# Retention queries and keys as block products, four group-norm roots at once on VectorE, and the output transposes in the next stage

## The chip, the cores and the metric

The kernel runs on one core of a Trainium2 chip. A core has TensorE (PE: matmuls and transposes, results in PSUM), VectorE (DVE), ScalarE (ACT), GpSimd (POOL) and SyncE (SP, which here only issues transfers); each works off a queue of its own in order, and semaphores join them. 16 DMA engines move data between HBM and the on-chip memory (SBUF). The metric is the time of one execution in microseconds of the device, smaller is better.

## The reference

Two layers of a hybrid decoder on 512 tokens of width 1024. Each layer has one combined input projection, dilated window attention in three groups, retention with four heads, sigmoid gates, an output projection and a SwiGLU block, with a LayerNorm after each half. What the change touches is retention:

```python
z = jnp.einsum('bsd,dc->bsc', x, w_in) + b_in          # q_r, k_r: 4 heads x 256 columns each
def rot(t):
    t1, t2 = t[..., :half], t[..., half:]
    return jnp.concatenate([t1 * cos - t2 * sin, t1 * sin + t2 * cos], axis=-1)
q = rot(q); k = rot(k) * (dk ** -0.5)
...
# o: per head a causal product of decayed scores (q k^T) with v, 512 columns a head
mu = jnp.mean(o, axis=-1, keepdims=True)
var = jnp.mean(jnp.square(o - mu), axis=-1, keepdims=True)
return (o - mu) * lax.rsqrt(var + GN_EPS)
...
y_b = jax.nn.silu(g_r) * y_r
```

## The kernel before

Every float32 operand of a large product is split into a high and a low part of a shorter format (`hilo`, L92: ScalarE casts the high part, VectorE subtracts to get the low part), and a product is three matmuls (`mm3`, L84): high by high, high by low, low by high. The activations x stand transposed in `xh` and `xl`, eight blocks of 128 rows by 512 tokens. Weights come in raw tiles of 128 x 1024 (`rawp`, eight of them, L64), loaded from the SyncE queue (L110, L211), and are split into pairs `whi`, `wlo` (`wp`, four pairs, L61).

Most projections are block products: the activations, the weights and the result are cut into 2 x 2 blocks, and seven products of sums of blocks do the work of eight. `Right` (L306) prepares the weight side: it loads B11, B21, B22 and the sums P1 = B11 + B12 and P3 = B12 + B22, whose second summand is added in flight by an accumulating transfer from GpSimd's queue (L321); P2 and P4 are made from P1 on VectorE (L347). The high parts are cast by ScalarE (L330) one product ahead, the low parts made by VectorE (L336). The sums of x for the left side stand in `xs`. `wide` (L406) runs the seven products with weights stationary and 256 tokens moving, into three PSUM tiles that `ev` empties; the merge gates of the layer (`gates`, L921) and most of the FFN use it. `tall` (L377) does the same with x stationary and 512 columns moving; the retention values and output gates of a head come from it through `biased` (L458).

Retention queries and keys were left as a plain product: `rotary(h)` (L657) loads two weight tiles each for q and k, multiplies with 512 tokens moving (`wstat`, L233), forms the products with the cosine and sine tables straight from PSUM (L668), adds them (L672, L673) and splits the result.

The stages of a head follow each other in the loop at L890: `rotary(h)`, then `ret_values_gates(h)`. Beside them run small jobs from a list, `side`: `pace(us)` spreads what is in the list over so many microseconds of matmuls, `tick` (L134) takes jobs out as the matmuls are written, and `drain` writes the rest. The scores of head h (`ret_scores`, L836) are side jobs of its values stage; its outputs (`ret_outputs`, L856) are side jobs of the next head's rotary stage, or of `gates` for the last head. One output job multiplies scores with values, takes mean and variance (L868, L869), the root (`rstd_of`, L120: a power on GpSimd and one Newton step on VectorE), subtracts the mean and multiplies by the gate (L872), and scales by the root on ScalarE (L873). A turn job transposes the four 128 x 128 parts on TensorE (L878), copies them out (L880) and writes them to HBM from ScalarE's queue (L881). `y_load` reads them back in the last call of `gates`.

The order in which instructions stand on an engine's queue is set when the program is built, by a planner that goes through the program with estimated durations and takes, when an engine is free, the earliest written instruction that is ready. So a weight's low part can stand ahead of an eviction that is written before it.

Of the kernel before, what the change touches and what calls it, by code (L numbers as in the profile page):

```python
# [10 lines left out]

F32 = mybir.dt.float32
F32R = mybir.dt.float32r
AF = mybir.ActivationFunctionType
ALU = mybir.AluOpType
PSUM = bass.MemoryType.PSUM
# [2 lines left out]
P = 128  # L19
# [3 lines left out]
NI = S // P  # L23
# [9 lines left out]
RQ = 256  # L33
# [4 lines left out]
C_QR = 3 * AW  # L38
C_KR = C_QR + RH * RQ
# [5 lines left out]
EPS = 1e-5  # L45
# [8 lines left out]
def hybrid_kernel(ctx, tc, x, rel_bias, w_in, b_in, w_attn_proj, w_ret_proj, w_out,  # L54
# [3 lines left out]
    pe, act, dve, pool = nc.tensor, nc.scalar, nc.vector, nc.gpsimd  # L58
# [25 lines left out]
    def mm3(ps, ah, al, bh, bl, start, stop):  # L84
        mm(ps, ah, bh, start, False)
        mm(ps, ah, bl, False, False)
        mm(ps, al, bh, False, stop)
# [4 lines left out]
    def hilo(src, hi, lo):  # L92
        act.copy(out=hi, in_=src)  # L93
        dve.tensor_tensor(out=lo, in0=src, in1=hi.bitcast(F32), op=ALU.subtract)  # L94
# [4 lines left out]
    def work(name):  # L99
        return wk.tile([P, S], F32, tag="w2", name=name)  # L100
# [4 lines left out]
    def view(t, a, b):  # L105
        return t[:, :a * b].rearrange("p (a b) -> p a b", a=a)
# [13 lines left out]
    def rstd_of(var):  # L120
        ve = sm.tile([P, 1], F32, tag="ve", name="ve")
        y = sm.tile([P, 1], F32, tag="ry", name="ry")
        t = sm.tile([P, 1], F32, tag="rt", name="rt")
        dve.tensor_scalar(ve, var, EPS, None, op0=ALU.add)
        pool.tensor_tensor(out=y, in0=ve, in1=mhalf, op=ALU.pow)  # L125
        dve.scalar_tensor_tensor(out=t, in0=y, scalar=ve, in1=y, op0=ALU.mult, op1=ALU.mult)
        dve.tensor_scalar(t, t, -0.5, 1.5, op0=ALU.mult, op1=ALU.add)
        dve.tensor_tensor(out=y, in0=y, in1=t, op=ALU.mult)
        return y


# [10 lines left out]
    def pace(us):  # L142
        rate[0], credit[0] = len(side) / us, 0.0
# [57 lines left out]
    def pair_units(w, c, c2=None):  # L201

        vs = []
        for hf in range(2):
            ks = slice(4 * hf, 4 * hf + 4)
            if c2 is None:
                vs.append(load(w[:, ks, c:c + 256], 4, 256))
            else:
                vs.append(view(raw(), 4, 256))
                for q, cc in enumerate((c, c2)):  # L210
                    nc.sync.dma_start(vs[hf][:, :, q * P:(q + 1) * P], w[:, ks, cc:cc + P])  # L211
        return [unit(v) for v in vs]
# [20 lines left out]
    def wstat(us, q):  # L233

        need(*range(NI))
        ps = psum("ps")
        for k in range(KD):
            h, l = part_of(us, k, q)
            mm3(ps, h, l, xh[:, k], xl[:, k], k == 0, k == KD - 1)
            tick(STEP)  # L240
        return ps
# [395 lines left out]
    def layer(ly, cp):  # L637
# [4 lines left out]
        def bcol(c):  # L642
            return bT[:, c // P:c // P + 1]
# [10 lines left out]
        def slot(name="op", dt=F32R):  # L654
            return opp.tile([P, 2, S], dt, tag="op", name=name)

        def rotary(h):  # L657

            rot = []
            for c0 in (C_QR + h * RQ, C_KR + h * RQ):  # L660
                us = pair_units(w_l, c0)
                prod = []
                for t in range(2):
                    ps = wstat(us, t)
                    pr = []
                    for tb in (cos, sin):
                        m = work("rp")
                        dve.scalar_tensor_tensor(out=m, in0=ps, scalar=bcol(c0 + t * P), in1=tb, op0=ALU.add, op1=ALU.mult)  # L668
                        pr.append(m)
                    prod.append(pr)  # L670
                (t1c, t1s), (t2c, t2s) = prod
                dve.tensor_tensor(out=t1c, in0=t1c, in1=t2s, op=ALU.subtract)  # L672
                dve.tensor_tensor(out=t1s, in0=t1s, in1=t2c, op=ALU.add)  # L673
                pair = []
                for src in (t1c, t1s):
                    o_ = slot("rot")
                    hilo(src, o_[:, 0], o_[:, 1])
                    pair.append(o_)
                rot.append(pair)
            heads[h]["q"], heads[h]["k"] = rot  # L680

        def ret_values_gates(h):
            cv, cg = C_VR + h * RV, C_GR + h * RV
            vr = heads[h]["v"] = [None] * NI
            gs = heads[h]["g"] = [None] * NI
            pairs = {}

            def left(i, ps, s):
                if s is not None:
                    dve.tensor_tensor(out=s, in0=ps, in1=s, op=ALU.add)  # L690
                vr[i] = slot("vr")
                hilo(ps if s is None else s, vr[i][:, 0], vr[i][:, 1])

            def gate(i, t):
                if i // 2 not in pairs:
                    pairs[i // 2] = slot("gs", F32)
                gs[i] = pairs[i // 2][:, i % 2]
                act.activation(out=gs[i], in_=t, func=AF.Silu)

            yield from biased(halves(w_l, 0, (2, 2), cv, cg, RV), RV, ly * RH + h, left, gate)  # L700
# [134 lines left out]
        with stage("ret") as rp:  # L835
            def ret_scores(h):  # L836

                dec = rp.tile([P, S], F32, tag="dec", name="dec")
                pool.dma_start(dec, c_dec[h])
                heads[h]["p"] = [rp.tile([P, 2, S - j * P], F32R, tag=f"p{j}", name="pj") for j in range(NI)]  # L840

                def one(j):
                    n = S - j * P
                    ps = psum()[:, :n]
                    for d in range(2):
                        k_, q_ = heads[h]["k"][d], heads[h]["q"][d]
                        mm3(ps, k_[:, 0, j * P:(j + 1) * P], k_[:, 1, j * P:(j + 1) * P],
                            q_[:, 0, j * P:], q_[:, 1, j * P:], d == 0, d == 1)
                    t = work("pt")
                    dve.tensor_tensor(out=t[:, :n], in0=ps, in1=dec[:, :n], op=ALU.mult)  # L850
                    sl = heads[h]["p"][j]
                    hilo(t[:, :n], sl[:, 0], sl[:, 1])

                return [lambda j=j: one(j) for j in range(NI)]

            def ret_outputs(h):  # L856

                ys = {}

                def one(i):  # L860
                    po = psum()
                    for j in range(i + 1):
                        sl, o = heads[h]["p"][j], (i - j) * P
                        vr = heads[h]["v"][j]
                        mm3(po, sl[:, 0, o:o + P], sl[:, 1, o:o + P], vr[:, 0], vr[:, 1], j == 0, j == i)
                    st = sm.tile([P, 6], F32, tag="st", name="st")
                    mv = sm.tile([P, 2], F32, tag="mv", name="mv")
                    dve.bn_stats(out=st, in_=po)  # L868
                    dve.bn_aggr(out=mv, in_=st)  # L869
                    rs = rstd_of(mv[:, 1:2])  # L870
                    y = ys[i] = rp.tile([P, RV], F32, tag="yb", name="yb", bufs=4)
                    dve.scalar_tensor_tensor(out=y, in0=po, scalar=mv[:, 0:1], in1=heads[h]["g"][i], op0=ALU.subtract, op1=ALU.mult)  # L872
                    act.mul(out=y, in_=y, mul=rs)  # L873

                def turn(i):
                    px = psum()
                    for t in range(NI):
                        pe.transpose(px[:, t * P:(t + 1) * P], ys[i][:, t * P:(t + 1) * P], ident)  # L878
                    o_ = work("yt")
                    act.copy(out=o_, in_=px)  # L880
                    act.dma_start(y_d[h * RV:(h + 1) * RV, i * P:(i + 1) * P].rearrange("(t p) s -> p t s", p=P),  # L881
                                  o_.rearrange("p (t s) -> p t s", t=NI))

                ops = [lambda i=i: one(i) for i in range(NI)]
                tr = [lambda i=i: turn(i) for i in range(NI)]
                n = [nothing]
                return ops[:1] + n * 2 + ops[1:2] + n * 2 + ops[2:3] + tr[:1] + n * 2 + ops[3:] + tr[1:2] + n * 3 \
                    + tr[2:3] + n * 4 + tr[3:]

            for h in range(RH):  # L890
                if h:
                    pace(20)
                    rotary(h)
                    drain()
                    vg = ret_values_gates(h)
                side.extend([nothing] * (8 if h else 1) + ret_scores(h))
                pace(14 if h == 0 else 30)
                run(vg)
                drain()
                side.extend(ret_outputs(h))  # L900


            wa_l, wr_l = rows(w_attn_proj[ly]), rows(w_ret_proj[ly])
# [302 lines left out]
```

## Time and profile before

| what | us |
|---|---|
| three runs | 2182.38, 2186.73, 2186.76; median 2186.73 |
| profiled execution, its own time | 2185.52 |
| span of its profile | 2183.7 |

The three retention heads with a rotary stage of this kind take, in layer 0, the time from 288.35 to 508.88 us of the span; layer 1 repeats it about 1080 us later. The profile's windows give, for a stretch of time, how long each engine was busy (with the number of instructions), the clock granted to TensorE as a share of full speed, the share of time that the DMA engines were busy, and GB/s. The timeline gives start, duration, engine, line, operation, output and inputs of each instruction, and in brackets how long the engine had been idle before it and what ended that. The chain of waits is followed back from the last instruction. A matmul's duration in a row is longer than its spacing from the next, since matmuls are pipelined.

### The profile page before, as it was taken

To read this page: it belongs to the slowest core of one execution; us is meant where nothing else is said; L and a number is where in the kernel's file an instruction comes from. 1 tells how busy PE (TensorE), PEld (TensorE's weight loads), DVE (VectorE), ACT (ScalarE), POOL (GpSimd) and SP (SyncE) were. 2 spreads that over 40 slices of the span, in tenths; PEclk is the share of its full clock that TensorE was granted. 3 is DMA by queue.
4 is the path that set the end of the run, shared out by engine and by line. 5 is a ranking of instruction groups with operands and counts; after the bars stand their busy time and mean duration, and the time that the engine had idled before them with its cause. 6 is when DMAs were issued, how large, how long until landed. Compare 5 with 4: busy or idle time off the path is not lost.

```text
span 2183.7 us, 32442 instructions
## 1 busy us (share of the span) xinstructions
PE 2161.5 (99%) x12906; PEld 1902.4 (87%) x12906; DVE 1396.0 (64%) x2011; ACT 980.6 (45%) x1585; POOL 228.3 (10%) x253
## 2 busy tenths in 40 slices
PE   8999999999999999999999999999999999999998
PEld 7977788889988899989898778888899889999996
DVE  5643677777755685747675346767877447766575
ACT  4444544546633263525245445444556233544350
POOL 4100011011000100010020000111010001000001
PEclk9999999999999999999999999999999999999999
DMA  8944266458685356656269343565577762666551
GB/s 230 235 134 104 59 164 164 135 131 194 190 305 192 88 154 132 171 133 158 93 163 255 89 92 92 140 178 148 137 188 227 260 193 58 175 151 161 125 161 39
DMA packets 304954, 338.60 MB, mean 155 GB/s; under 512 B 21790, under 2 KB 243138, under 8 KB 304673
## 3 DMA queue, kind: packets, MB, share of 16 engines
q1 hardware_dynamic: 227712, 248.81, 37.8%
q0 software_dynamic: 49808, 74.90, 18.1%
q10 hardware_dynamic: 27280, 12.80, 2.1%
q8 instruction: 101, 1.65, 0.3%
q14 instruction: 53, 0.43, 0.1%
HBM read 310.67 MB, written 28.53 MB: 155 GB/s over the span
## 4 chain that ended last, share of the span: by engine, by line
PE 90%; issue 4%; DMA 3%; DVE 2%; POOL 1%; ACT 0%; SPq 0%; POOLq 0%; DVEq 0%; ACTq 0%
PE ps L82 81%; PE px L82 7%; DMA raw<-in_w_in 2%; PE px L546 1%; DMA exd<-wb 1%; PE px L878 1%; POOL ry L125 0%; DMA mb<-exd 0%; DMA exd<-pk 0%; PE px L170 0%; DVE xtok L1001 0%; DVE wlo L336 0%; ACT whi L330 0%; PE px L602 0%; DVE xtok L1010 0%
## 5 line engine op out<-in xcount | busy, mean ns | idle before, releaser
L336 DVE TENSOR_TENSOR wlo<-raw,whi 128x1024 fp32r<-128x1024 f32 (+1 forms) x364 | 417.9, 1150 | 214.1 <-ACT whi L330 212.9
L82 PE MATMUL ps<-xh,whi 128*128 128x256 f32 (+1 forms) x1536 | 516.6, 338 | 4.5 <-ACT whi L93 3.5
L330 ACT CAST whi<-raw 128x1024 fp32r<-128x1024 f32 (+1 forms) x364 | 359.0, 990 | 345.4 <-PE ps L82 205.3
L82 PE MATMUL ps<-xh,wlo 128*128 128x256 f32 (+1 forms) x1536 | 500.9, 327 | 1.0 <-DVE wlo L94 1.0
L82 PE MATMUL ps<-xl,whi 128*128 128x256 f32 (+1 forms) x1536 | 501.2, 327 | 0.2 <-DVE xl L94 0.2
L82 PE MATMUL ps<-xs,whi 128*128 128x256 f32 (+1 forms) x2048 | 404.6, 296 | 0.0
L82 PEld LDWEIGHTS ps<-xs,whi 128*128 128x128 f32 x2048 | 327.7, 191 | 10.3
L94 DVE TENSOR_TENSOR wlo<-raw,whi 128x1024 fp32r<-128x1024 f32 (+2 forms) x162 | 193.3, 1196 | 202.0 <-ACT whi L93 201.0
L82 PEld LDWEIGHTS ps<-xh,whi 128*128 128x128 f32 x1536 | 292.4, 191 | 34.3 <-issue 5.7
L82 PEld LDWEIGHTS ps<-xh,wlo 128*128 128x128 f32 x1536 | 292.9, 191 | 26.5 <-DVE wlo L94 1.2
L82 PEld LDWEIGHTS ps<-xl,whi 128*128 128x128 f32 x1536 | 293.7, 191 | 19.5 <-DVE xl L94 1.0
L82 PE MATMUL ps<-xs,wlo 128*128 128x256 f32 (+1 forms) x1024 | 303.4, 296 | 0.0
L93 ACT CAST whi<-raw 128x1024 fp32r<-128x1024 f32 (+2 forms) x162 | 166.0, 1027 | 240.8 <-PE ps L82 150.7
L82 PE MATMUL ps<-whi,xs 128*128 128x512 f32 (+1 forms) x768 | 219.6, 360 | 0.6 <-ACT whi L330 0.4
L82 PEld LDWEIGHTS ps<-xs,wlo 128*128 128x128 f32 x1024 | 196.0, 191 | 5.0
L82 PE MATMUL ps<-whi,ht 128*128 128x512 f32 x576 | 178.4, 389 | 0.0
L82 PEld LDWEIGHTS ps<-whi,xs 128*128 128x128 f32 x768 | 137.7, 188 | 21.1 <-ACT sn L466 1.0
L82 PE MATMUL ps<-wlo,xs 128*128 128x512 f32 (+1 forms) x384 | 138.1, 360 | 0.8 <-DVE wlo L336 0.8
L321 POOL DMA_DIRECT2D raw<-in_w_in x64 | 79.2, 1263 | 472.9 <-DMA raw<-in_w_in 159.8
L82 PEld LDWEIGHTS ps<-whi,ht 128*128 128x128 f32 x576 | 108.2, 188 | 22.3
L321 POOL DMA_DIRECT2D raw<-in_w_ffn_gate x40 | 51.8, 1295 | 679.4 <-DMA raw<-in_w_ffn_up 251.4
L347 DVE TENSOR_TENSOR raw<-raw 128x1024 f32<-128x1024 f32 (+1 forms) x104 | 119.5, 1149 | 2.7 <-DMA raw<-in_w_in 0.5
(183 smaller groups left out, 2897.0 us busy)
## 6 DMA issues: line engine op xcount, KB each, us to landing
raw<-in_w_in SPq DMA_DIRECT2D x152, 512.0 KB, 4.3
raw<-in_w_ffn_up SPq DMA_DIRECT2D x64, 512.0 KB, 4.1
raw<-in_w_in POOLq DMA_DIRECT2D x48, 512.0 KB, 6.9
raw<-in_w_ffn_gate SPq DMA_DIRECT2D x44, 512.0 KB, 4.6
raw<-in_w_ffn_down SPq DMA_DIRECT2D x44, 512.0 KB, 4.2
raw<-in_w_ffn_gate POOLq DMA_DIRECT2D x40, 512.0 KB, 6.7
raw<-in_w_in SPq DMA_DIRECT2D x72, 256.0 KB, 4.9
raw<-in_w_ret_proj SPq DMA_DIRECT2D x32, 512.0 KB, 6.1
```

What stands on the lines that cost most here:

```text
L82: pe.matmul(ps, lhsT=a, rhs=b, start=start, stop=stop, skip_group_check=True)
L93: act.copy(out=hi, in_=src)
L94: dve.tensor_tensor(out=lo, in0=src, in1=hi.bitcast(F32), op=ALU.subtract)
L321: pool.dma_start(r, self.src({"P1": "B12", "P3": "B22"}[n], u), accum_op=ALU.add)
L330: act.copy(out=h, in_=src)
L336: dve.tensor_tensor(out=l, in0=src, in1=h.bitcast(F32), op=ALU.subtract)
L347: dve.tensor_tensor(out=r, in0=r, in1=self.t["B22" if n == "P2" else "B21", u], op=ALU.add)
L546: pe.transpose(px[:, (2 + j) * P:(3 + j) * P], s[:, hh, j * P:(j + 1) * P], ident)
L878: pe.transpose(px[:, t * P:(t + 1) * P], ys[i][:, t * P:(t + 1) * P], ident)
```

## The change

- `rotary(h)` for heads 1 to 3 becomes one block product through `wide`, with the head's query columns and key columns as the two column halves of the weights and tokens 0 to 255 and 256 to 511 as the two halves of x. `ev` copies products 1, 5, 6 and 4 out with the bias on ScalarE (two activations of 256 columns each), adds products 2, 7 and 3 to them on VectorE, and `turned` rotates each finished quarter, 128 x 2 x 256, in SBUF. Head 0 keeps the plain product.
- The rotated tiles are laid out anew: one tile holds the high parts of both halves of the head's columns, another the low parts.
- The mean and variance of a head's four outputs go into one tile, and `rstd_vector` takes the four roots together on VectorE, from a start value made of the number's bits and three Newton steps, twelve operations on four columns. The four scalings on ScalarE follow in a job `norms` behind the fourth output.
- The outputs of a head stay beside the next head's rotary stage (now 18 us of pace), its four transposes go into the values stage of that head, ahead of the scores. For the last head outputs and transposes all stand beside `gates`.
- The two gate tiles of a head are allocated at the start of its values stage rather than at their first use.

```diff
+    def rstd_vector(var, n):
+        ve, y, t, u = (sm.tile([P, n], F32, tag=f"nr{i}", name="nr", bufs=2) for i in range(4))
+        dve.tensor_scalar(ve, var, EPS, None, op0=ALU.add)
+        dve.tensor_scalar(y.bitcast(I32), ve.bitcast(I32), -0.5, 1597463007.0, op0=ALU.mult, op1=ALU.add)
+        dve.tensor_scalar(ve, ve, -0.5, None, op0=ALU.mult)
+        for _ in range(3):
+            dve.tensor_tensor(out=t, in0=y, in1=y, op=ALU.mult)
+            dve.tensor_tensor(out=u, in0=t, in1=ve, op=ALU.mult)
+            dve.scalar_tensor_tensor(out=y, in0=u, scalar=1.5, in1=y, op0=ALU.add, op1=ALU.mult)
+        return y
...
+        def turned(t, ts_, hi, lo):
+            n = t.shape[2]
+            s = view(work("rs"), 2, n)
+            cs, sn_ = (a[:, ts_].unsqueeze(1).to_broadcast([P, 2, n]) for a in (cos, sin))
+            dve.tensor_tensor(out=s, in0=t, in1=sn_, op=ALU.mult)
+            dve.tensor_tensor(out=t, in0=t, in1=cs, op=ALU.mult)
+            dve.tensor_tensor(out=t[:, 0], in0=t[:, 0], in1=s[:, 1], op=ALU.subtract)
+            dve.tensor_tensor(out=t[:, 1], in0=t[:, 1], in1=s[:, 0], op=ALU.add)
+            hilo(t, hi[:, :, ts_], lo[:, :, ts_])
...
+            def biased_copy(ps, c, sign=1.0):
+                o_ = view(work("sn"), 2, 256)
+                for q in range(2):
+                    act.activation(out=o_[:, q], in_=ps[:, q * 256:(q + 1) * 256], func=AF.Identity, bias=bcol(c + q * P), scale=sign)
+                return o_
+
+            def ev(i, ps):
+                p2 = ps.rearrange("p (q t) -> p q t", q=2)
+                if i in (1, 5):
+                    sn[i] = biased_copy(ps, cq if i == 1 else ck)
+                elif i == 6:
+                    sn[i] = biased_copy(ps, ck, -1.0)
+                elif i == 2:
+                    dve.tensor_tensor(out=sn[1], in0=p2, in1=sn[1], op=ALU.add)
+                    turned(sn[1], slice(0, 256), *heads[h]["q"])
+                elif i == 7:
+                    dve.tensor_tensor(out=sn[5], in0=sn[5], in1=p2, op=ALU.subtract)
+                    turned(sn[5], slice(256, 512), *heads[h]["k"])
+                elif i == 3:
+                    dve.tensor_tensor(out=sn[6], in0=p2, in1=sn[6], op=ALU.add)
+                    turned(sn[6], slice(0, 256), *heads[h]["k"])
+                elif i == 4:
+                    turned(biased_copy(ps, cq), slice(256, 512), *heads[h]["q"])
+
+            wide(pair_right(w_l[:, :, cq:], w_l[:, :, ck:], 0), x_left, ev)
...
+                mv = sm.tile([P, NI, 2], F32, tag="mv4", name="mv", bufs=2)
...
-                    rs = rstd_of(mv[:, 1:2])
...
-                    act.mul(out=y, in_=y, mul=rs)
+                def norms():
+                    rs = rstd_vector(mv[:, :, 1], NI)
+                    for i in range(NI):
+                        act.mul(out=ys[i], in_=ys[i], mul=rs[:, i:i + 1])
...
-                return ops[:1] + n * 2 + ops[1:2] + n * 2 + ops[2:3] + tr[:1] + n * 2 + ops[3:] + tr[1:2] + n * 3 \
-                    + tr[2:3] + n * 4 + tr[3:]
+                return ops[:1] + n * 2 + ops[1:2] + n * 2 + ops[2:3] + n * 3 + ops[3:] + n + [norms] + n, \
+                    n * 2 + tr[:1] + n + tr[1:2] + n + tr[2:3] + n + tr[3:]
 
             for h in range(RH):
                 if h:
-                    pace(20)
+                    side.extend(ops)
+                    pace(18)
                     rotary(h)
                     drain()
                     vg = ret_values_gates(h)
-                side.extend([nothing] * (8 if h else 1) + ret_scores(h))
+                    side.extend(turns + [nothing] * 2)
+                side.extend([nothing] + ret_scores(h))
                 pace(14 if h == 0 else 30)
                 run(vg)
                 drain()
-                side.extend(ret_outputs(h))
+                ops, turns = ret_outputs(h)
+            side.extend(ops + turns)
```

## Prediction: what the change does to the time

> **What bounds the kernel now.** First the page: shares of the engines and the chain that ended last.
>
> ```profile
> span 2183.7 us, 32442 instructions
> ...
> PE 2161.5 (99%) x12906; PEld 1902.4 (87%) x12906; DVE 1396.0 (64%) x2011; ACT 980.6 (45%) x1585; POOL 228.3 (10%) x253
> ...
> PE 90%; issue 4%; DMA 3%; DVE 2%; POOL 1%; ACT 0%; SPq 0%; POOLq 0%; DVEq 0%; ACTq 0%
> ```
>
> TensorE is busy for 99% of the span and 90% of the chain is its own work. So time is gained by fewer matmul microseconds, and lost where another engine comes late. Next, the waits of TensorE, of which one row concerns the low parts of weights that VectorE makes in the block products:
>
> ```profile
> PE ps L82 <- DVE wlo L336: 0.8, 2, 0.4
> ```
>
> In the whole kernel TensorE lost 0.8 us to them. Nothing is left to recover there, but it is the wait that the change can make grow. Then the windows by stage: rotary(2) of layer 0, values and gates of head 2, and one call of gates(), which already multiplies in the form that the change gives to rotary.
>
> ```profile
> 361.83:392.30 30.47, 30.47 (x143) 25.20 (x142) 21.14 (x44) 10.53 (x15) 7.07 (x8) 1.00 0.78 177
> 392.30:435.33 43.03, 43.03 (x197) 35.88 (x197) 33.16 (x40) 24.68 (x33) 0.62 (x1) 1.00 0.43 126
> ...
> 557.34:577.90 20.56, 20.56 (x174) 20.56 (x173) 13.52 (x14) 13.04 (x20) 1.29 (x1) 1.00 0.70 192
> ```
>
> Columns: length, PE, weight loads, DVE, ACT, POOL busy, clock, DMA share, GB/s. TensorE has no gap in any of the three and its clock is 1.00, so a stage's length is its count of matmuls times their spacing. One head takes 30.47 + 43.03 = 73.5 us, in which VectorE is busy 21.14 + 33.16 = 54.3 us.
>
> **The matmuls.** The spacing is read from the chain of waits in order of time:
>
> ```profile
> 317.18 0.44 PE px L878 x4
> 317.62 25.52 PE ps L82 x112
> 343.14 1.36 PE px L82 x6
> ...
> 511.89 6.11 PE ps L82 x51
> ```
>
> A matmul 512 wide takes 25.52 / 112 = 0.228 us (six score matmuls 1.36 / 6 = 0.227), one 256 wide 6.11 / 51 = 0.1198 us, four transposes 0.44 us. Test on the stages: rotary(2) holds 96 matmuls (q and k, two halves, 8 blocks, 3 passes), 30 of the outputs of the head before, and 16 transposes: 96 x 0.228 + 30 x 0.227 + 4 x 0.44 = 21.89 + 6.81 + 1.76 = 30.46 against 30.47. The call of gates(): 168 x 0.1198 + 0.44 = 20.57 against 20.56.
>
> The change puts 7 products x 2 x 4 x 3 = 168 matmuls 256 wide in place of the 96: 20.13 in place of 21.89 us, 1.76 us less for each of three heads in two layers, **10.6 us** in all. The transposes are moved, not removed: the new rotary stage needs 20.13 + 6.81 = 26.94 us of TensorE, the values stage 43.03 + 1.76 = 44.79 us, together 71.7 us instead of 73.5. Heads 0 keep their form.
>
> That each load serves only 256 columns shows in the window: weight loads are busy 20.56 of 20.56 us there, 25.20 of 30.47 in rotary. [...]
>
> **VectorE.** Its timeline in rotary(2), where the start of one row less the start of the row before is what an operation really costs:
>
> ```profile
> 375.98 0.22 DVE L126 SCALAR_TENSOR_TENSOR rt<-ry,ve 128x1 f32<-128x1 f32 x1 [6.04 <-POOL ry L125]
> ...
> 377.56 0.69 DVE L868 BATCH_NORM_STATS2 st<-px 128x6 f32<-128x512 f32 x1
> 378.29 0.18 DVE L869 BATCH_NORM_AGGREGATE mv<-st 128x2 f32<-128x6 f32 x1
> 378.50 0.15 DVE L124 TENSOR_SCALAR ve<-mv 128x1 f32<-128x1 f32 x1
> 378.57 0.74 DVE L872 SCALAR_TENSOR_TENSOR yb<-px,mv,gs 128x512 f32<-128x512 f32 x1
> 379.32 0.22 DVE L126 SCALAR_TENSOR_TENSOR rt<-ry,ve 128x1 f32<-128x1 f32 x1
> 379.57 0.15 DVE L127 TENSOR_SCALAR rt<-rt 128x1 f32<-128x1 f32 x1
> 379.76 0.16 DVE L128 TENSOR_TENSOR ry<-ry,rt 128x1 f32<-128x1 f32 x1
> 379.87 1.23 DVE L336 TENSOR_TENSOR wlo<-raw,whi 128x1024 fp32r<-128x1024 f32 x1
> 381.01 0.75 DVE L668 SCALAR_TENSOR_TENSOR rp<-ps,bT,cos 128x512 f32<-128x512 f32 x1
> 381.67 0.74 DVE L668 SCALAR_TENSOR_TENSOR rp<-ps,bT,sin 128x512 f32<-128x512 f32 x1
> 382.33 0.68 DVE L673 TENSOR_TENSOR rp<-rp 128x512 f32<-128x512 f32 x1
> 382.93 0.69 DVE L672 TENSOR_TENSOR rp<-rp 128x512 f32<-128x512 f32 x1
> 383.53 1.22 DVE L336 TENSOR_TENSOR wlo<-raw,whi 128x1024 fp32r<-128x1024 f32 x1
> 384.67 0.69 DVE L868 BATCH_NORM_STATS2 st<-px 128x6 f32<-128x512 f32 x1
> ```
> ```profile
> 351.47 0.41 DVE L850 TENSOR_TENSOR pt<-px,dec 128x256 f32<-128x256 f32 x1
> 351.80 1.22 DVE L336 TENSOR_TENSOR wlo<-raw,whi 128x1024 fp32r<-128x1024 f32 x1
> ```
>
> So 1024 columns cost 1.14 us, the two table products 0.66 each, a 512-column sum 0.60, a 256-column one 0.33, one output with its root 377.56 to 379.87 = 2.31, without the root's four operations (0.07 + 0.25 + 0.19 + 0.11) 1.69.
>
> Removed in a head: 4 low parts (4.56), 8 table products (5.28), 4 sums and 4 low parts of 512 (4.80), 4 outputs with roots (9.24): 23.9 us. Added: 7 low parts and 2 sums of 1024 for P2 and P4 (10.26), 3 sums of 512 on eviction (1.80), 4 rotations of 3 x 0.60 + 2 x 0.33 (9.84), 4 outputs without roots (6.76), and 12 dependent operations on four columns at about 0.2 (between the 0.25 and 0.11 of the rows): 2.4. That is 31.1 us, **7.2 us more per head**. The rotation with a broadcast table is not in the trace; a plain 0.60 and the 0.66 of the table product bound it, four heads' worth of that difference being half a microsecond; I take 0.60.
>
> Over a head VectorE then has 54.3 + 7.2 = 61.5 us of work in 71.7 us: it fits, at 86%. In the rotary stage alone it doesn't: 31.1 against 26.94 us. What lets it fit is lead: four pairs of weight tiles (wp, bufs=4), so low parts can be made three products, some 8.6 us, ahead. The queue by hand, from the first rotary matmul: by 13.8 us (the third output) VectorE owes five or six low parts, both sums and two outputs, about 13 us, and can be done with them. From there every eviction comes: output, product 2, product 7, output, product 3, roots, product 4, that is 1.69 + 3.06 + 3.06 + 1.69 + 3.06 + 2.4 + 2.46 = 17.4 us, and among them the low parts for the values stage, four of them (4.56) up to the second weight tile of its second product. All is done at 13.8 + 22.0 = 35.8 us. TensorE wants that tile at 26.94 + 0.23 + 24 x 0.228 + 6 x 0.228 = 34.0 us. That makes 1.8 us too late if the roots' gaps stay empty, and 0 to 0.4 if other work fills them or the planner pulls a low part ahead of a rotation; nothing waits for a rotation before the scores, some 25 us on. I take **0.5 us** per head, 3 us in all, nearer the lower end, because in the values stage of before VectorE already runs full for a while beside a TensorE without a gap:
>
> ```profile
> 325.00:330.00 5.00, 5.00 (x23) 4.13 (x22) 4.97 (x6) 2.56 (x4) 0.00 (x0) 1.00 0.00 0
> ```
>
> **Roots and transposes.** Before, a root is a GpSimd operation, and it stood behind a weight accumulation that waited for its load:
>
> ```profile
> 374.15 1.20 POOL L321 DMA_DIRECT2D raw<-in_w_in  x1 [4.69 <-issue]
> 374.90 1.04 POOL L125 TENSOR_TENSOR ry<-ve,mhalf 128x1 f32<-128x1 f32 x1
> ```
>
> VectorE, whose next operation needed that root, stood still for 6.04 us (the row at 375.98). TensorE didn't notice, so its end is worth nothing in itself; it gives back the idle time in which the lead above is built, and it matters because rotary now puts two more accumulations per head on that same GpSimd queue.
>
> The new wait: all four scalings of a head, and so all its transposes, wait for the fourth output. In ScalarE's queue behind a late scaling stand the weight casts, in TensorE's behind a late transpose the values' matmuls. By the queue above the roots are made between 27 and 31 us, the first transpose comes some 5.6 us into the values stage, at 32.5 us: a margin of 1 to 5 us, cost nothing. The four 256 KB writes to y_d move with the transposes, and with them their issues on ScalarE's queue, past the casts of the first two products; the DMA share there is 0.43 and nobody reads y_d before the last gates() call. For head 3 the order is outputs, roots, transposes over the same 40 us of gates() as before: nothing.
>
> **ScalarE and the transfers.**
>
> ```profile
> L330 ACT CAST whi<-raw 128x1024 fp32r<-128x1024 f32 x308 | 321.6, 1048 | 302.4 <-PE ps L82 178.3 <-issue 63.1 <-DVE raw L347 40.7
> ```
> ```profile
> q1 hardware_dynamic: 227712, 248.81, 37.8%
> q0 software_dynamic: 49808, 74.90, 18.1%
> ```
>
> ScalarE gets 3 more casts of 1.05 us and 8 biased copies of 256 columns. These are not in the trace; none is longer than a cast of 1024 or shorter than nothing, so at most 3.1 + 8.4 us, on 10.53 + 24.68 = 35.2 us per head: at most 46.7 of 71.7 us, hidden. The transfers of a head take 0.78 x 30.47 + 0.43 x 43.03 = 42.3 us of all 16 engines; one more load (0.378 x 2183.7 / 248.81 = 3.3 us per MB, 1.7 us) and two accumulations (0.181 x 2183.7 / 74.9 = 5.3 us per MB, 2.8 each) make 49.6 of 71.7: hidden, as long as the eight raw tiles come free in time. Rotary holds five of them now and the values stage wants ten. gates() after the values of head 3 starts with the same five, and its row above has no gap; the loads for the values stage start later by one tile's turn, with several products of 5.5 us to spare. If that cover is gone, it costs up to a load from issue to landing, once per head:
>
> ```profile
> raw<-in_w_in SPq DMA_DIRECT2D x152, 512.0 KB, 4.3
> ```
>
> **Sum.** Against the profiled execution's own 2185.52 us (1.2 us under the median of the runs): 2185.52 - 10.6 + 3.0 = **2178 us**, 0.34% faster. Each term but the 3.0 has no more than a microsecond of play.
>
> **Rivals.** (1) *VectorE paces the rotary stage* and the kernel gets slower. The stage then lasts 31.1 us in place of 30.47 and the values stage still takes the transposes, 1.76 us: 2.4 us more per head, 14 us, **2200 us**. It decides from the point where the low parts have no lead left, that is if the planner sets every rotation ahead of the next product's low part or the weight tiles come free too late. For it: 31.1 against 26.94. Against: the four pairs of tiles, the rows at 379.87 and 383.53, where a low part for a stage still to come is made between outputs and rotations, and the 10 us that VectorE has to spare per head. (2) *The crunch at the end of rotary costs its full 1.8 us* or a little more: the saving is eaten, 2185.5 - 10.6 + 6 x 1.8 = **2186 us**, between 2181 and 2190. For it: the twelve roots' operations depend on each other, and rotations precede the values' weights in the program. (3) *Loads come late*: 4.3 us per head less the 1.76, 2185.5 + 6 x 2.5 = **2201 us**; against it the 49.6 of 71.7 us. (4) *All is hidden*: 2185.5 - 10.6 = **2175 us**; that is the forecast's lower end, not a case of its own.
>
> **From these to the numbers.** Forecast with its lower end, 2173 to 2181: 0.55. Rival 2: 0.25, of which 0.03 falls under 2181. Rival 1 with anything in between from 2190 on: 0.16. Rival 3: 0.04. The measurement can tell about 0.2% from no change, 4.4 us, so faster means under 2182, slower over 2191. Faster 0.57, same 0.25, slower 0.18. The range runs from 2172.5 (the runs of before lie up to 3 us under the profiled one, and the saving may be whole) to 2193, which leaves out most of rival 1 and rival 3. The likeliest case by itself: 2173 to 2181.
>
> **What would show it.** Right: rotary windows of heads 1 to 3 near 27 us, values windows near 45, 0.12 us spacing in rotary, VectorE near 61 us per head without long idle times, the row of TensorE's waits for low parts at a few us. Wrong: that row at 10 us or more (rival 2 at 11, rival 1 at 25), and its place tells which: at the start of the values stage it is rival 2, within rotary's products rival 1. Waits of ScalarE's casts for raw tiles would be rival 3. Waits of TensorE for a scaling would mean that the transposes' margin was wrong, and a spacing other than 0.12 us that the matmul term was.

## The result and the profile after

| kernel | median, us | runs | least to most, us |
|---|---|---|---|
| before | 2185.64 | 4 | 2182.38 to 2186.76 |
| changed | 2201.24 | 4 | 2195.49 to 2202.40 |

The changed kernel takes 1.0064 times as long (95% interval 1.0049 to 1.0078). The prediction was 2178, with a range to 2193; the change is slower by 14 us by this ratio (15.6 by the medians), and the forecast had the wrong sign. The profiled execution took 2202.4 us. First its page: span, busy time of the engines, chain of work that ended last.

```profile
span 2200.6 us, 33442 instructions
...
PE 2158.3 (98%) x13338; PEld 1919.0 (87%) x13338; DVE 1433.1 (65%) x2051; ACT 1017.5 (46%) x1651; POOL 225.3 (10%) x233
...
PE 86%; DVE 5%; issue 4%; DMA 3%; ACT 1%; POOL 1%; SPq 0%; POOLq 0%; ACTq 0%; DVEq 0%
```

There are 432 more matmuls, as 6 x (168 - 96) should make, and TensorE was busy 3.2 us less than before (2161.5). It was idle 42.3 us (2200.6 - 2158.3) where it was idle 22.2 us before (2183.7 - 2161.5). VectorE's share of the chain has gone from 2% to 5%. The waits of TensorE say for whom it stood still (in all, times, longest, in us):

```profile
PE px L929 <- ACT yb L924: 17.8, 6, 3.0
...
PE ps L83 <- DVE wlo L350: 0.4, 1, 0.4
```

L929 is the first transpose of a head's outputs, L924 the scaling by the root. Six heads, six waits of 3.0 us: 17.8 of the 20.1 us of added idle time. The row that the prediction feared, low parts of weights, stands at 0.4 us, lower than the 0.8 before. Where in a head the time lies shows in the windows of rotary(1) and of the values stage behind it (length, PE, weight loads, DVE, ACT, POOL busy, clock, DMA share, GB/s):

```profile
289.68:316.69 27.01, 27.01 (x199) 25.75 (x198) 23.45 (x36) 11.70 (x18) 5.13 (x5) 1.00 0.80 192
316.69:366.30 49.61, 46.64 (x214) 38.59 (x213) 37.13 (x59) 29.91 (x43) 3.18 (x3) 0.97 0.57 150
```

Rotary takes 27.01 us without a gap; 26.94 were forecast. The values stage takes 49.61 instead of the forecast 44.79: 2.97 us of it TensorE stands idle, and its busy time is 46.64, 1.85 more than forecast, at a clock of 0.97. Now VectorE's timeline from the first of the root's operations (L136 to L142, `rstd_vector`) to the last:

```profile
316.75 0.16 DVE L136 TENSOR_SCALAR nr<-mv 128x4 f32<-128x4 f32 x1
316.82 1.22 DVE L350 TENSOR_TENSOR wlo<-raw,whi 128x1024 fp32r<-128x1024 f32 x1
317.96 0.68 DVE L677 TENSOR_TENSOR sn<-sn,cos 128x512 f32<-128x512 f32 x1
318.56 0.16 DVE L137 TENSOR_SCALAR nr<-nr 128x4 int32<-128x4 int32 x1
318.64 0.69 DVE L676 TENSOR_TENSOR rs<-sn,sin 128x512 f32<-128x512 f32 x1
...
324.50 0.15 DVE L142 SCALAR_TENSOR_TENSOR nr<-nr 128x4 f32<-128x4 f32 x1
324.57 1.22 DVE L350 TENSOR_TENSOR wlo<-raw,whi 128x1024 fp32r<-128x1024 f32 x1
325.70 0.15 DVE L140 TENSOR_TENSOR nr<-nr 128x4 f32<-128x4 f32 x1
325.78 0.68 DVE L95 TENSOR_TENSOR rot<-sn,rot 128x512 fp32r<-128x512 f32 x1
326.38 0.15 DVE L141 TENSOR_TENSOR nr<-nr 128x4 f32<-128x4 f32 x1
326.45 0.68 DVE L741 TENSOR_TENSOR sn<-ps,sn 128x512 f32<-128x512 f32 x1
327.05 0.15 DVE L142 SCALAR_TENSOR_TENSOR nr<-nr 128x4 f32<-128x4 f32 x1
```

Each of the twelve operations takes only 0.07 us of the queue (316.75 to 316.82), but all but one of them are followed by other work, a low part or a piece of a rotation, before their successor. So 0.9 us of work lasts from 316.75 to 327.12, 10.4 us, without an idle moment on VectorE. What waited, on ScalarE and on TensorE:

```profile
327.17 0.62 ACT L94 CAST vr<-sn 128x512 fp32r<-128x512 f32 x1 [2.24 <-DVE sn L741]
327.69 2.56 ACT L924 ACTIVATE yb<-yb,nr 128x512 f32<-128x512 f32 x4
```
```profile
325.11 0.39 PE L83 MATMUL ps<-whi,xl 128*128 128x512 f32 x1
328.46 0.66 PE L929 MATMUL px<-ident,yb 128*128 128x128 f32 x4 [2.97 <-ACT yb L924]
```

TensorE reaches the first transpose in its queue after the matmul of 325.11. The scalings start at 327.69, the transpose at 328.46, and the values' matmuls behind it, which need nothing from the outputs, wait too.

### The profile page after: what moved, and what is told of

The parts are those of the page before. It is cut to its first block, busy times and chain, and to the rows that moved or that the text cites. A ratio compares the mean times of both kernels' runs of the same rounds, so it can differ in the third digit from the quotient of the medians.

```text
span 2200.6 us, 33442 instructions
## 1 busy us (share of the span) xinstructions
PE 2158.3 (98%) x13338; PEld 1919.0 (87%) x13338; DVE 1433.1 (65%) x2051; ACT 1017.5 (46%) x1651; POOL 225.3 (10%) x233
## 4 chain that ended last, share of the span: by engine, by line
PE 86%; DVE 5%; issue 4%; DMA 3%; ACT 1%; POOL 1%; SPq 0%; POOLq 0%; ACTq 0%; DVEq 0%
PE ps L83 77%; PE px L83 7%; DMA raw<-in_w_in 1%; DVE wlo L350 1%; DMA exd<-wb 1%; PE px L560 1%; PE px L929 1%; DVE rot L95 1%; POOL ry L126 0%; DMA mb<-exd 0%; DMA exd<-pk 0%; PE px L184 0%; DVE xtok L1055 0%; DVE rs L676 0%; ACT whi L344 0%
## 5 line engine op out<-in xcount | busy, mean ns | idle before, releaser
L350 DVE TENSOR_TENSOR wlo<-raw,whi 128x1024 fp32r<-128x1024 f32 (+1 forms) x406 | 469.4, 1158 | 249.3 <-ACT whi L344 247.1
L344 ACT CAST whi<-raw 128x1024 fp32r<-128x1024 f32 (+1 forms) x406 | 404.8, 999 | 454.9 <-PE ps L83 252.1
L83 PE MATMUL ps<-xh,whi 128*128 128x256 f32 (+1 forms) x1488 | 479.8, 324 | 3.7 <-ACT whi L94 2.4
L83 PE MATMUL ps<-xs,whi 128*128 128x256 f32 (+1 forms) x2432 | 474.1, 294 | 0.0
L83 PE MATMUL ps<-xh,wlo 128*128 128x256 f32 (+1 forms) x1488 | 465.7, 314 | 1.0 <-DVE wlo L95 1.0
L83 PE MATMUL ps<-xl,whi 128*128 128x256 f32 (+1 forms) x1488 | 466.3, 314 | 0.2 <-DVE xl L95 0.2
L83 PEld LDWEIGHTS ps<-xs,whi 128*128 128x128 f32 x2432 | 388.5, 191 | 11.3
L83 PE MATMUL ps<-xs,wlo 128*128 128x256 f32 (+1 forms) x1216 | 357.7, 294 | 0.0
L95 DVE TENSOR_TENSOR wlo<-raw,whi 128x1024 fp32r<-128x1024 f32 (+2 forms) x138 | 164.0, 1191 | 189.7 <-ACT whi L94 189.1
L83 PEld LDWEIGHTS ps<-xs,wlo 128*128 128x128 f32 x1216 | 232.8, 191 | 5.0
```

The costliest lines, as they stand in the source:

```text
L83: pe.matmul(ps, lhsT=a, rhs=b, start=start, stop=stop, skip_group_check=True)
L344: act.copy(out=h, in_=src)
L350: dve.tensor_tensor(out=l, in0=src, in1=h.bitcast(F32), op=ALU.subtract)
```

## The experiments

The theory after the result: **late scalings**. The matmul saving is there, but the root's chain ends some 3 us after TensorE has reached the first transpose. The rival: **VectorE's load** of 7 us more per head makes everything that hangs on it late, and the transposes are only where that first shows. Each kernel was timed beside the kernel before on the same chip. The diffs are against the changed kernel unless said otherwise.

### The transposes later

```diff
-                    side.extend(turns + [nothing] * 2)
+                    side.extend([nothing] * 8 + turns + [nothing] * 2)
```

> The changed kernel with eight empty jobs more ahead of the transposes in the values stage, nothing else. Late scalings (the twelve root operations are strung out between large VectorE operations, so the scalings and the first transposes come 3 us too late, and TensorE stands still behind them): the first transpose now stands some 5 us later in TensorE's queue, its wait for a scaling falls from 17.8 us in the kernel to under 2 us, the half clock after the gaps goes too, and the time is that of before less the 10.6 us of the matmuls, about 2175 to 2178 us. VectorE's load (31 us of work in a rotary stage of 27): its work is the same, so the time stays at 2195 to 2202 us and the wait only changes its place.

Measured: 2175.80 us (five runs, 2175.1 to 2177.27), ratio to before 0.9952 (0.9940 to 0.9965), beside 2186.5 for the kernel before. VectorE's work is the same. The page, and the windows of the same head:

```profile
span 2173.9 us, 33452 instructions
...
PE 2150.9 (99%) x13338; PEld 1913.2 (88%) x13338; DVE 1431.7 (66%) x2051; ACT 1014.3 (47%) x1651; POOL 225.4 (10%) x233
```
```profile
288.30:315.32 27.02, 27.02 (x199) 25.75 (x198) 23.45 (x36) 11.71 (x18) 5.13 (x5) 1.00 0.81 198
315.32:360.06 44.74, 44.74 (x214) 37.30 (x213) 36.83 (x58) 29.26 (x43) 3.18 (x3) 1.00 0.64 163
```

No wait for a scaling is left. 27.02 + 44.74 = 71.76 us a head; the prediction had 71.7. VectorE is busy 60.28 of them (predicted 61.5), TensorE has no gap at a clock of 1.00. So VectorE's load as such costs nothing here, and the rival falls. The gain of 10.7 us against before is the matmul term, 10.6.

A quarter of that delay, two empty places instead of eight:

```diff
-                    side.extend(turns + [nothing] * 2)
+                    side.extend([nothing] * 2 + turns + [nothing] * 2)
```

> The changed kernel with two empty places ahead of the four transposes in the values stage, a quarter of the eight of the run with late transposes. The first transpose moves 12 matmuls, 2.7 us, down TensorE's queue. Late scalings: of the 3.0 us gap about 0.3 us is left per head, and a gap this short leaves the clock alone: 2176 to 2179 us. If more hangs on the transposes than the wait for the roots (their copies or writes crowding the start of the values stage), the time stays above 2185 us.

Measured: 2179.11 us (2177.47 to 2180.57), ratio 0.9974 (0.9963 to 0.9985). The wait is

```profile
PE px L929 <- ACT yb L924: 2.4, 6, 0.4
```

0.4 us per head instead of 3.0. Twelve more matmuls of 0.228 us, 2.7 us, now stand ahead of the transpose. A gap of this length stands in the profile of before too, 0.39 us ahead of 1164.79, and over the five microseconds behind it the clock was 1.00.

### The length of the chain

These two kernels leave every instruction on TensorE's queue where the changed kernel has it, and change only the number of Newton steps.

```diff
-        for _ in range(3):
+        for _ in range(2):
```

> The changed kernel with two Newton steps instead of three in the four roots of a head (less exact roots): nine dependent operations on VectorE instead of twelve, and every instruction on TensorE's queue in the place where the changed kernel has it. Late scalings: the roots end some 2.5 us earlier (three operations of about 0.15 us, each followed by a foreign operation of 0.6 to 1.2 us), so the 3.0 us wait of TensorE for a scaling in each of six heads shrinks to between 0 and 0.7 us and the slow clock behind it goes: 2176 to 2182 us. Rival, VectorE's load in the rotary stage as such makes it late, whoever is at the end of its queue: three tiny operations (0.45 us of work per head) less change little, the gap stays at 2.5 us or more, 2195 to 2201 us.

Measured: 2177.99 us (2174.56 to 2180.86), ratio 0.9969 (0.9958 to 0.9980). Timeline of VectorE, the last root operation, and of TensorE:

```profile
325.07 0.15 DVE L142 SCALAR_TENSOR_TENSOR nr<-nr 128x4 f32<-128x4 f32 x1
```
```profile
325.67 0.39 PE L83 MATMUL ps<-whi,xl 128*128 128x512 f32 x1
326.17 0.66 PE L929 MATMUL px<-ident,yb 128*128 128x128 f32 x4
```

The transpose follows its forerunner by 0.50 us instead of 3.35. Three operations of 0.07 us less gave 23 us. And one step more:

```diff
-        for _ in range(3):
+        for _ in range(4):
```

> The changed kernel with four Newton steps instead of three (roots more exact than asked): fifteen dependent operations, TensorE's queue order unchanged. Late scalings: the roots end some 2.5 us later, the wait of TensorE for a scaling grows from 3.0 to about 5 or 5.5 us in each of six heads, so 12 to 15 us longer than the changed kernel, 2211 to 2220 us, and the clock falls behind every one of the six gaps. Rival, the work of the operations counts and not their places in the queue: 0.45 us more per head, 2203 to 2205 us.

Measured: 2223.71 us (2223.18 to 2227.77), ratio 1.0185 (1.0170 to 1.0200). Page and waits:

```profile
span 2221.7 us, 33466 instructions
...
PE 2165.3 (97%) x13338; PEld 1924.0 (87%) x13338; DVE 1435.3 (65%) x2075; ACT 1018.8 (46%) x1651; POOL 225.3 (10%) x233
```
```profile
PE px L929 <- ACT yb L924: 33.7, 6, 5.6
```

The wait came out close to the expectation, 5.6 us a head and 15.9 more in all. The total is above the expected range: the span is 21.1 us longer than the changed kernel's, because TensorE's busy time also grew, by 7.0 us for the same matmuls. That is the clock, 0.71 to 0.86 over the ten microseconds behind the six gaps (last section). The rival's 2 to 4 us is far off: it is the place of the operations in the queue that counts, not their work.

### The parts of the change

The old root for each output on GpSimd, and its scaling at once, with the rest of the change as it is:

```diff
-                def norms():
-                    rs = rstd_vector(mv[:, :, 1], NI)
-                    for i in range(NI):
-                        act.mul(out=ys[i], in_=ys[i], mul=rs[:, i:i + 1])
+                    rs = rstd_of(mv[:, i, 1:2])
...
+                    act.mul(out=y, in_=y, mul=rs)
...
-                return ops[:1] + n * 2 + ops[1:2] + n * 2 + ops[2:3] + n * 3 + ops[3:] + n + [norms] + n, \
+                return ops[:1] + n * 2 + ops[1:2] + n * 2 + ops[2:3] + n * 3 + ops[3:] + n * 3, \
```

> The changed kernel with the roots taken singly again, on GpSimd with one Newton step, each output scaled at once; block products and the late transposes stay. Late scalings: no string of twelve operations is left, the scalings are done when the transposes come unless GpSimd's queue holds a root up behind an accumulation; TensorE's wait for a scaling under 3 us, 2175 to 2181 us. VectorE's load: 2.3 us of root operations in place of 2.4 us per head, so 2195 us or more.

Measured: 2177.18 us (2175.33 to 2177.58), ratio 0.9956 (0.9943 to 0.9970), no wait for a scaling. It can't be told from the kernel with late transposes (which stand eight empty places later there), so the four roots at once show no gain that can be measured, even where they are not late.

The block products alone, with single roots, and the transposes among the outputs and the scores where they were before (diff against the run above):

```diff
-                return ops[:1] + n * 2 + ops[1:2] + n * 2 + ops[2:3] + n * 3 + ops[3:] + n * 3, \
-                    n * 2 + tr[:1] + n + tr[1:2] + n + tr[2:3] + n + tr[3:]
+                return ops[:1] + n * 2 + ops[1:2] + n * 2 + ops[2:3] + tr[:1] + n * 2 + ops[3:] + tr[1:2] + n * 3 \
+                    + tr[2:3] + n * 4 + tr[3:]
...
-                    side.extend(turns + [nothing] * 2)
-                side.extend([nothing] + ret_scores(h))
+                side.extend([nothing] * (8 if h else 1) + ret_scores(h))
...
-                ops, turns = ret_outputs(h)
-            side.extend(ops + turns)
+                ops = ret_outputs(h)
+            side.extend(ops)
```

> Block products alone: single roots and the transposes in the old places among the outputs. Late scalings: 2175 to 2181 us, with the transposes' waits of before (none). VectorE's load: the 31 us of work in the rotary stage remain and the stage has 1.8 us of transposes more for TensorE, so the kernel is as slow as the changed one less at most the transposes' shift, 2190 us or more. If GpSimd's roots come late behind the two further accumulations, waits of VectorE for roots grow and this kernel is slower than the one with late transposes.

Measured: 2182.45 us (2179.25 to 2188.07), ratio 0.9984 (0.9973 to 0.9995). Here low parts do come late:

```profile
PE ps L83 <- DVE wlo L350: 4.3, 4, 1.7
...
PE ps L83 <- ACT whi L344: 1.3, 2, 0.7
...
PE ps L83 <- DVE sn L723: 1.0, 1, 1.0
```

6.6 us in all. Beside the profile of before TensorE's busy time falls by 8.7 us (2161.5 to 2152.8), its idle time grows by 5.0 (22.2 to 27.2), and 3.7 us remain between the spans; the ratio gives a gain of 3.5 us (0.0016 of 2186). The time lies just above the 2181 of the first expectation and well under the 2190 of the second, and neither named these waits of TensorE. Beside the run before it, which differs in the order of the side jobs alone, the ratios are 0.0028 apart, 6 us. In the moved places the scores, too, have lost the empty places ahead of them; the runs don't part these.

And the other way round, plain queries and keys, with roots and transposes of the change:

```diff
-            if h == 0:
+            if True:
...
-                    pace(18)
+                    pace(20)
```

> The four roots at once and the late transposes, with queries and keys of all heads as plain products. Late scalings: the string of roots finds a VectorE with 7 us less work per head and is shorter, but it still begins behind the fourth output; a wait of 0 to 1.5 us per head, 2185 to 2194 us. VectorE's load: nothing is overloaded, so the time of before, 2183 to 2187 us, and no waits for scalings.

Measured: 2186.81 us (2182.86 to 2190.82), ratio 1.0004 (0.9995 to 1.0013), no wait for a scaling. The moves alone bring nothing; they are worth something only beside the block products, and the late scalings need the block products as well. Both expectations hold this time, and the missing wait is what the rival said. VectorE's timeline shows what the load has to do with it, the first and the last root operation and the row behind them:

```profile
314.37 0.16 DVE L136 TENSOR_SCALAR nr<-mv 128x4 f32<-128x4 f32 x1
...
316.40 0.16 DVE L142 SCALAR_TENSOR_TENSOR nr<-nr 128x4 f32<-128x4 f32 x1
316.51 1.23 DVE L350 TENSOR_TENSOR wlo<-raw,whi 128x1024 fp32r<-128x1024 f32 x1
```

Here nothing stands between the twelve, and the same chain lasts 2.1 us instead of 10.4. So the rival is right in one half: it is VectorE's other work that stretches the chain. It is wrong in the other: the same work costs nothing when the transposes come late enough.

### Head 0 too

The kernel with late transposes, and in it

```diff
-            if h == 0:
+            if False:
```

> The run with late transposes, and head 0 made as a block product as well, in both layers. If the matmul term holds for a head without outputs beside it, 2 x 1.76 = 3.5 us less than that run, 2171 to 2173 us. Rival: head 0 has no outputs of a head before it beside its queries and keys, so TensorE needs only 20 us there while VectorE has its 24 us of low parts, sums, evictions and rotations (31.1 less the outputs and roots), and the 4 us come back as waits for low parts: 2175 to 2180 us, no better.

Measured: 2177.01 us (2175.68 to 2182.58), ratio 0.9971 (0.9961 to 0.9982): no better. The time is the rival's, the reason is neither's. TensorE's largest wait, and behind it VectorE's row in layer 0:

```profile
PE px L616 <- DVE y L611: 10.1, 2, 5.5
```
```profile
266.75 0.69 DVE L611 TENSOR_TENSOR y<-y,fa 128x512 f32<-128x512 f32 x1 [5.67 <-DMA fa<-exd]
```

Head 0's stage also carries the end of the window attention, whose weights go through HBM and back (fa). TensorE got to the transposes behind that exchange at 262.1 us (in the kernel with late transposes at 266.23, without a wait), and VectorE's row above comes at 266.75 (there at 264.91). So TensorE waited, 5.45 us up to 267.58, and behind the wait its matmuls came every 0.43 us (268.89, 269.32); its clock was 0.88 over the stretch from 244.5 to 273 us. Then these transposes were put later, with two more products of the values stage written ahead of the point where the side jobs are drained (diff against the run above):

```diff
-            side.extend(n * 3 + tail[:1] + n * 8 + tail[1:2] + n + tail[2:3] + n + tail[3:4] + n * 3 + tail[4:5] + n * 7 + tail[5:6] + n * 2 + tail[6:])
+            side.extend(n * 3 + tail[:1] + n * 8 + tail[1:2] + n + tail[2:3] + n + tail[3:4] + n * 3 + tail[4:5] + n * 7 + tail[5:6] + n * 2 + [nothing] * 14 + tail[6:])
...
-            for _ in range(4):
+            for _ in range(6):
```

> The run with head 0 as a block product too, and the last transposes of the window attention's output, on which TensorE waited there for 5.5 and 4.6 us, set later in head 0's values stage (two more products of that stage are written ahead of the point where the side jobs are drained, and fourteen empty places stand ahead of the last transposes). If those waits are all that ate the saving of head 0, they go, 2177.0 less 3 to 10 us: 2167 to 2174 us. Rival: head 0's scores now have two products less to stand beside, and what was a wait for the exchange comes back as waits beside the scores: 2175 to 2180 us, no better than the kernel with late transposes.

Measured: 2169.34 us (2165.64 to 2171.82), ratio 0.9925 (0.9911 to 0.9939), the best of this study.

```profile
PE px L616 <- DVE y L611: 3.9, 2, 2.0
```

Of the 10.1 us, 3.9 are left. And the same place with head 0 as a plain product:

```diff
-            if False:
+            if h == 0:
```

> The run before this one with head 0 back as a plain product; its late place for the last transposes of the window attention stays. It parts the 6.5 us by which that run beat the kernel with late transposes. If the block product of head 0 is worth its 2 x 1.76 = 3.5 us there, this run lies 3.5 us above it, at 2172 to 2174 us, and the later place gives the other 3 us. If the later place only undid what head 0's block product had cost, this run is back at 2175 to 2177 us, the time of the kernel with late transposes.

Measured: 2174.45 us (2173.04 to 2177.90), ratio 0.9940 (0.9926 to 0.9953), between the two expectations. The ratios put head 0's block products at 0.0015, 3.3 us, the medians at 5.1 us; the forecast 3.5 lies between. But the intervals of the two runs overlap (0.9911 to 0.9939, 0.9926 to 0.9953), so this gain is not shown clear of the noise. What the later place gives by itself, 0 to 3 us, stays open as well: its interval overlaps that of the kernel with late transposes, whose trace has no wait for the exchange that a later place could remove.

## Why the prediction was wrong

**The failed step** is the wait of the transposes behind the roots: "By the queue above the roots are made between 27 and 31 us, the first transpose comes some 5.6 us into the values stage, at 32.5 us: a margin of 1 to 5 us, cost nothing." In the trace of after the roots start at 316.75, 27.1 us after the first rotary matmul at 289.68: right. They end at 327.2, 37.5 us after it: 6.5 us later than forecast. The first transpose would have come at 325.3, 35.7 us after it, later than forecast as well, which gave 3 us back. The scaling in between takes the transpose to 328.46. So the margin was minus 3 us where it was to be 1 to 5. The cause is in the sum of VectorE's queue: it took the roots as a block of 2.4 us ("12 dependent operations on four columns at about 0.2"). That is their length where nothing stands between them (2.1 us with plain queries and keys), but beside the block products the queue holds low parts and rotations between them, and the chain lasts 10.4 us. The prediction even counted on other work filling the gaps of the roots, as a help for the low parts, and did not follow what that does to the roots. With the chain three operations shorter the loss is gone, with three more the kernel is 38 us slower than before, and a later place for the transposes removes it: this cause is shown.

**The price** of that step: 2.97 us in each of six heads, 17.8 us, and a slow clock behind some of the gaps. Beside the profile with late transposes the span of after is 26.7 us longer (2200.6 - 2173.9), 19.3 of it idle time of TensorE and 7.4 busy time. Of the 7.4, 3.7 lie behind the gaps of two heads: 1.90 us in the values stage of head 1 (46.64 - 44.74), and 1.8 for head 2 (a clock of 0.91 from 400 to 420 us). Another 3.4 have nothing to do with this step: they lie in earlier stages of both layers, from 80 to 100 us (clock 0.91) and from 1160 to 1200 us (0.96), where the profile with late transposes has 1.00. So the step's own price in this profile is 17.8 + 3.7 = 21.5 us.

**The matmul term**, 10.6 us, was right: 27.02 and 44.74 us for the two stages, 10.7 us of gain in the run with late transposes. Its sum for VectorE over a head was right too, 60.3 us against 61.5 forecast, with 0.9 us for the roots where 2.4 were put. Its split was not: VectorE is busy 23.45 us in the rotary stage, not 31.1, and does the rest in the values stage.

**The crunch** at the end of rotary was put at 0.5 us a head, 3.0 in all; in the changed kernel the wait for low parts is 0.4 us in all. The mechanism exists: with the block products alone it is 4.3 us. Rivals 1 and 2 did not decide: both have their place in that row. That rival 1 named 2200 us and rival 3 2201, beside 2201.24 measured, is chance: rotary takes 27.01 us, not 31.1, and TensorE has no wait for a cast of these weights (L344). One of the prediction's sums is off in the last digit, and nothing rests on it: its chances for faster add up to 0.58, not 0.57.

**GpSimd's root.** The prediction held that removing VectorE's stand behind it mattered because it gives the idle time for the lead. With the old roots and the moved transposes the kernel is as fast as without (2177.18 us beside 2175.80): it didn't matter.

**ScalarE and the transfers** were hidden as argued: ScalarE is busy 40.97 us a head of the run with late transposes (at most 46.7 forecast), the transfers 0.81 x 27.02 + 0.64 x 44.74 = 50.5 us (49.6 forecast).

The prediction's last section named this sign: waits of TensorE for a scaling mean that the transposes' margin was wrong.

## What to carry to other kernels

A chain of tiny dependent operations on a busy engine does not cost its busy time: it costs its length in the queue, here over ten times as much (10.4 us for 0.9), because other work is put between its links. With nothing between them, as with plain queries and keys, it took 2.1 us; no run here keeps the links together beside the block products. Before moving a consumer behind such a chain, write down when the last link can end, with a foreign operation between every two, and when the in-order engine reaches the consumer; then put enough independent work ahead of it, which was free here (eight empty places on a list were worth 25 us). A faster stage also brings forward whatever else stands in it (with head 0 as a block product too, TensorE reached the transposes behind the exchange at 262.1 us instead of 266.23): look for the transfers that its old length hid.

## What the hardware showed

The clock of TensorE fell to half behind some gaps and not behind others of the same length. From after, the five microseconds behind the gaps of 2.97 us of heads 1, 2 and 3 of layer 0, and the matmuls behind the second gap:

```profile
328.46:333.46 5.00, 5.00 (x19) 4.15 (x20) 2.80 (x3) 3.79 (x6) 0.00 (x0) 0.66 0.18 52
405.12:410.12 5.00, 5.00 (x20) 4.21 (x21) 2.05 (x3) 3.77 (x6) 0.00 (x0) 0.70 0.12 34
481.60:486.60 5.00, 5.00 (x26) 4.20 (x27) 3.38 (x4) 4.74 (x7) 0.00 (x0) 1.00 0.20 57
```
```profile
406.45 0.63 PE L83 MATMUL ps<-wlo,xh 128*128 128x512 f32 x1
406.88 0.63 PE L83 MATMUL ps<-whi,xl 128*128 128x512 f32 x1
...
409.54 0.39 PE L83 MATMUL ps<-whi,xh 128*128 128x512 f32 x1
409.76 0.39 PE L83 MATMUL ps<-wlo,xh 128*128 128x512 f32 x1
```

Matmuls come every 0.43 us in the slow stretch (granted clock 0.50 from 405.20 to 408.00), 0.22 behind it. Two of the six gaps of 2.97 us had such a stretch, all three of layer 1 none. With the gaps of 5.6 us of the run with four Newton steps, the clock fell behind all six: over the ten microseconds behind them it was 0.85, 0.71, 0.81, 0.72, 0.81 and 0.86. The first two:

```profile
330.67:340.67 10.00, 10.00 (x44) 8.36 (x45) 3.65 (x4) 6.43 (x10) 0.00 (x0) 0.85 0.44 116
409.75:419.75 10.00, 10.00 (x38) 8.29 (x39) 3.74 (x4) 5.39 (x9) 0.00 (x0) 0.71 0.39 106
```

A clock of 0.85 over 10 us is 3.0 us at half speed, 0.71 is 5.8 us. That explains why four steps cost more than their wait. In the runs of after, too, the time goes with the clock: the three at 2201 to 2202 us had a mean clock of 0.995 to 0.996, the one at 2195.49 us had 0.998.

Slow stretches came behind shorter gaps as well. In after TensorE stood idle for 1.6 us in an earlier stage of each layer, here in layer 0:

```profile
86.38 0.40 PE L83 MATMUL ps<-whi,xs 128*128 128x288 f32 x1 [1.59 <-ACT sn L480]
```

The granted clock was 0.50 from 88 to 90 us, and behind the gap of 1.60 us before 1178.31 it was 0.50 from 1180 to 1182 us. In the run with late transposes the gap at the first of these places was 1.08 us, and the clock stayed at 1.00.

Behind which gaps the clock falls, no run here settles: a slow stretch came behind the gap of 1.59 us above, and none behind four of the six gaps of 2.97 us.
